# Spreading reciprocal roots over the partitions by transposition, and half 1's column sums by transposition and VectorE, in an encoder layer

## The chip, the cores and the metric

The kernel runs on one core of one Trainium2 chip. The metric is device time in microseconds (us). Lower is better. One profiled execution of the kernel before is at hand as well; all times below are microseconds from the start of its span unless they are marked ns.

## The reference

One layer of a bidirectional encoder over 1024 tokens of width 1024, in float32. What matters here are its two norms:

```
def rmsnorm(x, gain):
    xf = x.astype(jnp.float32)
    y = xf * lax.rsqrt(jnp.mean(xf * xf, axis=-1, keepdims=True) + EPS)
    return (y * gain.astype(jnp.float32)).astype(x.dtype)

h = rmsnorm(x, norm1_g) * (1.0 + sc1) + sh1
z = h @ w_in              # two branches (a gated MLP, a windowed attention) and two gates follow
...
x = x + gt1 * (merged @ w_o)
h2 = rmsnorm(x, norm2_g) * (1.0 + sc2) + sh2
f_gate, f_up = jnp.split(h2 @ w_ffn_in, 2, axis=-1)
x = x + gt2 * ((jax.nn.silu(f_gate) * f_up) @ w_ffn_out)
```

Each norm needs, for every token, the sum of the squares of its 1024 channels, the reciprocal root of their mean, and that root multiplied onto all 1024 channels of the token.

## The kernel before

The activations lie transposed: channels on the 128 partitions (eight tiles of 128 channels), tokens on the free axis. The 1024 tokens are worked in two halves of 512, by `half(0)` and `half(1)`; after them come the gates, the output projection, the second norm and the feed-forward part for both halves together. Nearly all products are "float32 as two parts": a high and a low part of each operand, three products (`mm3`: high by high, high by low, low by high).

Because channels lie on the partitions, the sum of squares of a token is a sum across partitions, and the root of a token must come back to all partitions. The steps of one norm for 512 tokens:

1. The squares of the eight channel tiles are added on ScalarE and VectorE into one 128 x 512 tile (`ss`).
2. `col_rstd` (line 381) takes the column sums on TensorE: for each of the four blocks of 128 tokens a float32 product with the block of `ss` as stationary operand and one column of ones as moving operand. A 128 x 4 tile comes out: token on the partition, block on the free axis.
3. `rstd` (line 375) turns it into the mean plus epsilon on VectorE (tile `ms`), and raises it to the power of minus one half on GpSimd (tile `rcol`).
4. `spread` (line 388) brings the root back to all partitions: for each block a float32 product whose stationary operand is the root's column repeated 128 times and whose moving operand is the identity. A 128 x 512 tile in PSUM comes out in which every partition holds all 512 roots.
5. VectorE multiplies the channel tiles with it (in `modulate`, line 409, and its like), ScalarE adds the shift and makes the high part, VectorE the low part.

The norms run at four places:

- **Norm 1 of half 0**, at the very start (lines 690 to 745). The column sums come there from products with a full tile of ones; the spread is written out, four float32 products into `rp`. Behind it in TensorE's program stand eight products for the condition's first column (`dot1`, into the bank `tot4`), then the projections' products. Half 0's attention window also reaches 128 tokens of the other half (the halo), which have a root of their own: `tot4[:, P : 2 * P]` at line 894 is its single product, issued ahead of the last pass of step k = 3; VectorE multiplies the halo's channels with it at k = 4 (`halo_four`).
- **Norm 1 of half 1**, inside half 0's last stage: the loop over d (eight tiles of output channels) with two groups of products j = 0, 1 per d, twelve matmuls each (lines 1169 to 1245). Behind group (4, 1) stands `col_rstd(ssn, NT, rcol[1])`, behind group (5, 0) `rb = spread(rcol[1], NT)`; in d = 5, 6, 7 `modulate` makes half 1's input from it.
- **Norm 2 of half 0** and **norm 2 of half 1**: column sums and `spread(rcol[2], NT)` out of a planner's list (lines 1780 to 1830; the planner, class `Plan`, orders operations by fixed costs, 0.45 for "few", the cost of a spread), and `col_rstd(sums[1], NT, rcol[3])` with `spread(rcol[3], NT)` among the first feed-forward products (lines 2153 to 2159).

Order: where `in_order[0]` is true, instructions keep their program order on each engine; elsewhere the framework's scheduler orders them (in half 0's last loop from d = 2 on, among other places). The last part runs under a manual schedule. TensorE, VectorE, ScalarE and GpSimd each work their queue in order.

The names in the profile: `at` and `mm` are the two sets of four PSUM banks, `mid`, `h`, `wh`, `wl`, `raw`, `t`, `ss`, `ms` SBUF tiles; all compute instructions carry line 144, a helper's line, and are told apart by tile names. `at<-ident,rcol` are the products of the spreads, `at<-ones,ss` the column sums, `at<-ident,lb`, `at<-ident,kd` and `at<-ident,mid` float32 transpositions that the kernel has elsewhere. A group's name gives the moving operand first, then the stationary one.

Of the kernel before, what the change touches and what calls it, by code (L numbers as in the profile page):

```python
# [16 lines left out]
P = 128  # L17
# [89 lines left out]
def kernel(  # L107
# [65 lines left out]
    def at_bank():  # L173
        return psum.tile([P, 512], F32, tag="at", name=nm("at"))
# [17 lines left out]
    def sm(n, name):  # L192
        return small.tile([P, n], F32, tag=name, name=nm(name))
# [184 lines left out]
        V.tensor_scalar(ms[:, :n], sums, 1.0 / D, EPS, op0=ALU.mult, op1=ALU.add)  # L378
        G.tensor_tensor(r[:, :n], ms[:, :n], nhalf[:, :n], op=ALU.pow)

    def col_rstd(ss, n, r):

        pt = at_bank()
        for i in range(n):
            T.matmul(pt[:, i : i + 1], ss[:, i * P : (i + 1) * P], ones[:, 0:1], start=True, stop=True)
        rstd(pt[:, :n], n, r)

    def spread(r, n):

        bc = at_bank()  # L390
        for i in range(n):
            T.matmul(bc[:, i * P : (i + 1) * P], r[:, i : i + 1].to_broadcast([P, P]), ident,
                     start=True, stop=True)
        return bc[:, : n * P]

    def ss_tile():
# [253 lines left out]
    def half(hf):  # L650
# [4 lines left out]
        if hf == 0:  # L655
            in_order[0] = True
            xt2 = [midt(F32, 4) for _ in range(2)]
            xt = [xt2[k // 4][:, k % 4, :] for k in range(KT)]
            halo = midt(F32, 16)
            xh, qh = halo[:, :KT, :], halo[:, KT:, :]  # L660
            hl4 = midt(F32R, 16)

            for k, n in ((0, 2), (2, 2), (4, 2), (6, 1), (7, 1)):
                load(xt2[k // 4][:, k % 4 : k % 4 + n, :].rearrange("p a b -> p (a b)"),
                     xA[:, k * HALF : (k + n) * HALF])
                if k == 2:
                    load_cond()
            hd_store = lambda q, f: f(
                hd[0, q * HALF : (q + 1) * HALF, :].rearrange("(a p) t -> p a t", p=P), xt2[q])
            load(cc[:, :80], cols)  # L670
            r = ada_pair(0)
            wq0, wk0 = (wpool.tile([P, UNIT], F32, tag="raw", name=nm("raw")) for _ in range(2))
            r1 = midt(F32, 2)
            load(r1[:, 0, :], blocks(w_ada1[1])[0])
            wq_half, wk_half = (blocks(w[0]) for w in (w_q, w_kv))
            load(wq0[:, :512], wq_half[0])
            load(wk0[:, :512], wk_half[0])
            load(r1[:, 1, :], blocks(w_ada1[1])[1])
            load(wq0[:, 512:], wq_half[1])
            base_bias = bias_base()  # L680
            A.activation(sm(QPK, "es"), ones[:, :QPK], AF.Silu)
            build_bias(*base_bias, range(BIAS))

            total = at_bank()
            open_bank(total, zeros, zeros)
            keep_going(total, zeros, zeros, ZEROS[0])
            cond = silu_rows()
            sqs = [midt(F32, 4) for _ in range(2)]
            sq = [sqs[k // 4][:, k % 4, :] for k in range(KT)]
            add = lambda i, j: V.tensor_tensor(sq[i], sq[i], sq[j], op=ALU.add)  # L690
            square = lambda k: A.activation(sq[k], xt[k], AF.Square)

            def square_dve(k):
                V.tensor_tensor(sq[k], xt[k], xt[k], op=ALU.mult)

            def column_sums(q, last=False):

                for i in range(NT):
                    T.matmul(total[:, i * P : (i + 1) * P], q[:, i * P : (i + 1) * P], ones,
                             start=False, stop=last and i == NT - 1)  # L700

            square(0)
            square(1)
            add(0, 1)
            column_sums(sq[0])
            square(2)
            square_dve(3)
            add(2, 3)
            column_sums(sq[2])
            square_dve(5)  # L710
            square(4)
            silu_cond(cond[:1])
            add(4, 5)
            column_sums(sq[4])
            square(6)
            square_dve(7)
            silu_cond(cond[1:], 1)
            A.activation(silu_col, ccol, AF.Silu)
            add(6, 7)
            column_sums(sq[6], True)  # L720
            root = sm(5, "ms")
            A.activation(root[:, :NT], total.rearrange("p (a b) -> p a b", b=P)[:, :, 0], AF.Sqrt, scale=1.0 / D, bias=epsc)
            wq, wk = ([wpool.tile([P, UNIT], F32R, tag=x, name=nm(x)) for x in ("wh", "wl")]
                      for _ in range(2))
            ada_dot(r[:, 0, :], SC1, then=ada_base)
            V.reciprocal(rcol[0][:, :NT], root[:, :NT])
            ada_dot(r[:, 1, :], SH1)
            rp = at_bank()
            kbk = [at_bank() for _ in range(2)]
            for bank in kbk:  # L730
                open_bank(bank, identr, zeros)
            keep_going(kbk[0], identr, zeros, ZEROS[1])
            for i in range(NT):
                T.matmul(rp[:, i * P : (i + 1) * P], rcol[0][:, i : i + 1].to_broadcast([P, P]), ident,
                         start=True, stop=True)
            tot4 = at_bank()

            dot1 = tot4[:, 2 * P : 3 * P]
            for i in range(KT):
                T.matmul(dot1, r1[:, 0, i * P : (i + 1) * P], silu_col[:, i : i + 1].to_broadcast([P, P]),  # L740
                         start=i == 0, stop=i == KT - 1)
            hH = [hid(), hid()]
            hL = [hid(), hid()]
        else:
            hH, hL = h_next
            in_order[0] = True
# [7 lines left out]
        for k in range(KT):  # L754
# [119 lines left out]
            for group in ((q_parts, k_parts) if hf == 1 and k == 4 else (q_parts + k_parts,)):  # L874


                if hf == 0:
                    if k == 4:
                        passes, late = [(e, q_parts) for e in range(3)], [(e, k_parts) for e in range(3)]
                    elif k == 0:  # L880
                        passes, late = [(0, group), (2, group), (1, q_parts)], [(1, k_parts)]
                    else:
                        passes, late = [(0, q_parts)] + late + [(0, k_parts), (1, group), (2, group)], []
                elif k == 0:

                    passes = [(e, part) for part in (q_parts[:3], q_parts[3:], k_parts) for e in (None, 2)]
                else:
                    passes = ((None, group), (2, group))
                for p, (e, part) in enumerate(passes):
                    if (hf, k, p) == (0, 2, 1):  # L890
                        for a in range(KT):
                            T.matmul(tot4[:, 0:1], qh[:, a, :], ones[:, 0:1], start=a == 0, stop=a == KT - 1)
                    elif (hf, k, p) == (0, 3, len(passes) - 1):
                        T.matmul(tot4[:, P : 2 * P], rcol[0][:, NT:].to_broadcast([P, P]), ident,
                                 start=True, stop=True)
                    for ps, st, w, o, n, first, last in part:
                        for e1 in ((0, 1) if e is None else (e,)):
                            T.matmul(ps, st[e1 // 2], w[e1 % 2][:, o : o + n],
                                     start=k + e1 == 0 and first,
                                     stop=bool(k == KT - 1 and e1 == 2 and last))  # L900
# [269 lines left out]
        for d in range(KT):  # L1170
# [24 lines left out]
            for j, (o, br) in enumerate(((512, (oH, oL)), (0, (gH, gL)))):  # L1195
                pb = mm_bank()
                for k in range(4):
                    kc = slice(o + k * P, o + (k + 1) * P)
                    mm3(pb, (wab[0][:, kc], wab[1][:, kc]),
                        (br[0][:, k, :], br[1][:, k, :]), k == 0, k == 3)  # L1200
                if hf == 0 and (d, j) == (4, 1):
                    col_rstd(ssn, NT, rcol[1])
                if hf == 0 and (d, j) == (5, 0):
                    rb = spread(rcol[1], NT)
                if d < PLAIN_GATES:
                    sg = sgs.pop(0)
                    V.scalar_tensor_tensor(out=sg, in0=sg, scalar=1.0, in1=pb, op0=ALU.add, op1=ALU.mult)
                    if (d, j) == (0, 0):
                        sums_of_w_o(3)
                    ms.append(sg)  # L1210
                else:
                    p = tmp()
                    A.copy(p, pb)
                    store(pd[hf, d, 1 - j], p)
# [1204 lines left out]
```

## Time and profile before

| | |
|---|---|
| median of 3 runs | 1214.48 us (1214.31 to 1214.61) |
| span of the profiled execution | 1212.9 us |
| median less span | 1.6 us |
| TensorE (PE) busy | 1206.9 us, 100% of the span, 5653 matmuls |
| TensorE weight loads (PEld) busy | 1007.5 us, 83% |
| VectorE (DVE) busy | 928.7 us, 77% |
| ScalarE (ACT) busy | 584.2 us, 48% |
| GpSimd (POOL) busy | 156.3 us, 13% |
| share of the 16 DMA engines | q1 39.5%, q0 16.2% |

The profile gives no time of its own for the profiled execution beside its span; the median of the runs lies 1.6 us above it. How to read it: a timeline's row gives start, duration, engine, line, operation, output tile and input tiles, shapes, the number of merged instructions and, in brackets, how long the engine had been idle before and what ended that. Matmuls overlap, so what a batch costs is the distance from its first start to the next group's start, not its duration. The chain of waits follows the end of the program back to its start, at each step to what released it.

### The profile page before, as it was taken

Reading aid. Unit: us, or ns where it says so; the run is one execution under the profiler, and the core shown is the slowest. Engines: PE = TensorE matmul, PEld = TensorE weight load, DVE = VectorE, ACT = ScalarE, POOL = GpSimd, SP = SyncE. Lnnn points to the kernel's source line nnn. Section 1 sums busy time; section 2 is a strip of 40 time slices with the busy share of each in tenths; the row PEclk is TensorE's granted clock in tenths of the full one; section 3 lists DMA queues with packets and bytes.
Section 4 is the critical chain, followed back from the end, with each engine's and each line's share of the span. In section 5 each row is a group of like instructions: output and inputs, shape, how many; then the busy total and the mean of one; then the engine's idle time right before and its main releaser. Section 6 shows DMA issues by size and latency. Waiting matters only on the chain.

```text
span 1212.9 us, 15658 instructions
## 1 busy us (share of the span) xinstructions
PE 1206.9 (100%) x5653; PEld 1007.5 (83%) x5653; DVE 928.7 (77%) x1505; ACT 584.2 (48%) x957; POOL 156.3 (13%) x190
## 2 busy tenths in 40 slices
PE   9999999999999999999999999999999999999998
PEld 7888888888888888888888888888888888888887
DVE  9999977889978886898987757676676765765646
ACT  5667865367855433745553333333333334433341
POOL 0024323024322000001000000010000000000001
PEclk9999999999999999999999999999999999999999
DMA  9743168753278543577213545554555449995552
GB/s 372 280 181 101 36 222 311 296 211 136 74 259 278 209 141 104 171 227 270 99 59 113 180 177 208 189 195 161 197 192 201 156 163 372 394 354 191 192 172 105
DMA packets 79713, 241.00 MB, mean 199 GB/s; under 512 B 9106, under 2 KB 9362, under 8 KB 74388
## 3 DMA queue, kind: packets, MB, share of 16 engines
q1 hardware_dynamic: 64004, 165.55, 39.5%
q0 software_dynamic: 15632, 74.46, 16.2%
q8 instruction: 44, 0.72, 0.2%
q14 instruction: 33, 0.27, 0.1%
HBM read 178.63 MB, written 61.34 MB: 198 GB/s over the span
## 4 chain that ended last, share of the span: by engine, by line
PE 99%; ACT 0%; DVE 0%; issue 0%; ACTq 0%
PE mm L144 50%; PE at L144 49%; DVE mid L144 0%; ACT mid L144 0%; ACT wh L144 0%; ACT h L144 0%; DVE crow L144 0%; ACT mod L144 0%; DVE zeros L144 0%; DVE ones L144 0%; DVE identr L144 0%; ACTq L144 0%
## 5 line engine op out<-in xcount | busy, mean ns | idle before, releaser
L144 ACT CAST wh<-raw 128x1024 fp32r<-128x1024 f32 (+1 forms) x154 | 157.1, 1021 | 110.7 <-PE mm L144 43.8
L144 DVE TENSOR_TENSOR wl<-raw,wh 128x1024 fp32r<-128x1024 f32 (+1 forms) x141 | 165.1, 1174 | 51.6 <-ACT wh L144 51.1
L144 PE MATMUL mm<-mid,wh 128*128 128x512 f32 x640 | 197.5, 390 | 0.0
L144 PEld LDWEIGHTS mm<-mid,wh 128*128 128x128 f32 x640 | 119.8, 188 | 24.7
L144 PE MATMUL mm<-wh,h 128*128 128x512 f32 x384 | 124.7, 396 | 0.2 <-ACT h L144 0.2
L144 PE MATMUL mm<-mid,wl 128*128 128x512 f32 x320 | 124.5, 389 | 0.0
L144 PE MATMUL mm<-h,wh 128*128 128x512 f32 x304 | 94.4, 391 | 0.0
L144 PE MATMUL at<-h,wh 128*128 128x512 f32 x304 | 93.8, 390 | 0.0
L144 PEld LDWEIGHTS mm<-wh,h 128*128 128x128 f32 x384 | 70.8, 188 | 13.9 <-ACT h L144 0.4
L144 DVE TENSOR_TENSOR wl<-ws,wh 128x1024 fp32r<-128x1024 f32 (+1 forms) x50 | 55.8, 1117 | 24.1 <-ACT wh L144 24.1
L144 PE MATMUL mm<-wl,h 128*128 128x512 f32 x192 | 71.2, 391 | 0.0
L144 PEld LDWEIGHTS mm<-mid,wl 128*128 128x128 f32 x320 | 60.1, 188 | 12.5
L144 PEld LDWEIGHTS at<-h,wh 128*128 128x128 f32 x304 | 56.9, 188 | 11.7
L144 ACT CAST wh<-ws 128x1024 fp32r<-128x1024 f32 (+1 forms) x50 | 48.3, 967 | 37.3 <-DVE ws L144 24.9
L144 PEld LDWEIGHTS mm<-h,wh 128*128 128x128 f32 x304 | 56.6, 188 | 11.6
L144 ACT ACTIVATE t<-t 128x512 f32<-128x512 f32 x46 | 28.4, 630 | 70.8 <-DVE t L144 70.8
L144 DVE TENSOR_TENSOR ol<-raw,oh 128x1024 fp32r<-128x1024 f32 x30 | 36.6, 1223 | 31.1 <-ACT oh L144 31.1
L144 PE MATMUL mm<-h,wl 128*128 128x512 f32 x152 | 59.2, 390 | 0.0
L144 PE MATMUL at<-h,wl 128*128 128x512 f32 x152 | 59.1, 389 | 0.0
L144 ACT ACTIVATE xs<-xs 128x512 f32<-128x512 f32 x21 | 13.3, 633 | 93.6 <-DVE xs L144 93.6
L144 ACT CAST oh<-raw 128x1024 fp32r<-128x1024 f32 x30 | 31.6, 1055 | 44.3 <-PE at L144 23.0
L144 PE MATMUL at<-wl,wh 128*128 128x512 f32 (+1 forms) x136 | 52.7, 388 | 0.0
(300 smaller groups left out, 2883.9 us busy)
## 6 DMA issues: line engine op xcount, KB each, us to landing
mid<-in_w_ada_dram SPq DMA_DIRECT2D x30, 512.0 KB, 7.4
raw<-in_w_gate_dram SPq DMA_DIRECT2D x26, 512.0 KB, 3.6
tA<-hid POOLq DMA_DIRECT2D x11, 1024.0 KB, 5.1
tB<-hid POOLq DMA_DIRECT2D x11, 1024.0 KB, 5.2
wo<-in_w_out_dram POOLq DMA_DIRECT2D x22, 512.0 KB, 6.1
wS<-wo POOLq DMA_DIRECT2D x11, 1024.0 KB, 5.2
raw<-wS SPq DMA_DIRECT2D x44, 256.0 KB, 3.5
raw<-tB SPq DMA_DIRECT2D x44, 256.0 KB, 5.0
```

Source lines behind the costliest of these rows:

```text
L144: ins = f(*args, **kw)
```

## The change

`T.transpose` takes the place of the float32 product in all spreads: in `spread`, in the one written out for `rp`, and in the halo's single one. It has the same operands: the root's repeated column, and the identity. That is 17 products of 128 x 128 in all (four in `rp`, one in `tot4`, four in each of three spreads).

Half 1's column sums are no longer products with ones. `turned` transposes the four 128 x 128 blocks of `ssn` into a PSUM bank, `summed` adds each block's 128 elements per partition by a `tensor_reduce` on VectorE (tile `cs`), and `rstd` reads that. The other column sums stay products. The spread of half 1's root is moved: from behind group (5, 0) to behind the first three matmuls of group (5, 1).

```diff
+    def turned(ss, n):
+
+        pt = at_bank()
+        for i in range(n):
+            T.transpose(pt[:, i * P : (i + 1) * P], ss[:, i * P : (i + 1) * P], ident)
+        return pt
+
+    def summed(pt, n):
+
+        s = sm(5, "cs")
+        V.tensor_reduce(out=s[:, :n], in_=pt[:, : n * P].rearrange("p (a b) -> p a b", b=P), axis=AX.X,
+                        op=ALU.add)
+        return s[:, :n]
+
-    def col_rstd(ss, n, r):
+    def col_rstd(ss, n, r, by_turning=False):

+        if by_turning:
+            rstd(summed(turned(ss, n), n), n, r)
+            return
         pt = at_bank()
         for i in range(n):
             T.matmul(pt[:, i : i + 1], ss[:, i * P : (i + 1) * P], ones[:, 0:1], start=True, stop=True)
...
         bc = at_bank()
         for i in range(n):
-            T.matmul(bc[:, i * P : (i + 1) * P], r[:, i : i + 1].to_broadcast([P, P]), ident,
-                     start=True, stop=True)
+            T.transpose(bc[:, i * P : (i + 1) * P], r[:, i : i + 1].to_broadcast([P, P]), ident)
         return bc[:, : n * P]
...
             for i in range(NT):
-                T.matmul(rp[:, i * P : (i + 1) * P], rcol[0][:, i : i + 1].to_broadcast([P, P]), ident,
-                         start=True, stop=True)
+                T.transpose(rp[:, i * P : (i + 1) * P], rcol[0][:, i : i + 1].to_broadcast([P, P]), ident)
...
-                        T.matmul(tot4[:, P : 2 * P], rcol[0][:, NT:].to_broadcast([P, P]), ident,
-                                 start=True, stop=True)
+                        T.transpose(tot4[:, P : 2 * P], rcol[0][:, NT:].to_broadcast([P, P]), ident)
...
+                    if hf == 0 and (d, j, k) == (5, 1, 0):
+                        rb = spread(rcol[1], NT)
                 if hf == 0 and (d, j) == (4, 1):
-                    col_rstd(ssn, NT, rcol[1])
-                if hf == 0 and (d, j) == (5, 0):
-                    rb = spread(rcol[1], NT)
+                    col_rstd(ssn, NT, rcol[1], True)
```

## The prediction

> **What bounds the kernel now.** I read the page first, for the bound of the whole, and then the waits of TensorE's two queues.
>
> ```profile
> span 1212.9 us, 15658 instructions
> ...
> PE 99%; ACT 0%; DVE 0%; issue 0%; ACTq 0%
> ...
> PE at L144 <- DVE identr L144: 1.9, 1, 1.9
> PE mm L144 <- ACT h L144: 0.2, 1, 0.2
> ```
>
> The chain that ended last is TensorE for 99% of the span, and TensorE waits twice: 1.9 us before its first matmul, and 0.2 us for ScalarE's `h`. So each matmul that goes away is worth its place in TensorE's stream, unless another engine is just as late at that point. The change removes only matmuls from the stream. Two questions remain: what is a transposition worth against a product, and where does TensorE, come earlier, meet something that doesn't come earlier with it?
>
> The price is read from timelines, as the distance from one group's first start to the next group's. Half 1's column sums and its spread:
>
> ```profile
> 188.51 0.94 PE L144 MATMUL at<-ones,ss 128*128 128x1 f32 x8
> 189.31 0.72 PE L144 MATMUL mm<-mid,wh 128*128 128x512 f32 x2
> ...
> 189.49 0.16 DVE L144 TENSOR_SCALAR ms<-at 128x4 f32<-128x4 f32 x1 [2.74 <-PE at L144]
> 189.57 1.23 DVE L144 TENSOR_TENSOR wl<-raw,wh 128x1024 fp32r<-128x1024 f32 x1
> ...
> 189.74 1.96 POOL L144 TENSOR_TENSOR rcol<-ms,nhalf 128x4 f32<-128x4 f32 x1 [2.17 <-DVE ms L144]
> ...
> 192.18 1.05 PE L144 MATMUL at<-ident,rcol 128*128 128x128 f32 x8
> 192.99 0.71 PE L144 MATMUL mm<-mid,wh 128*128 128x512 f32 x2
> ```
>
> Four float32 products are eight instructions, two passes each. The column sums hold the stream from 188.51 to 189.31, 0.80 us, and the spread from 192.18 to 192.99, 0.81 us: 0.10 us a pass, with one column as with 128. The kernel's own transpositions of float32 blocks, four of `kd` and sixteen of `mid`, with the group behind each:
>
> ```profile
> 66.03 0.60 PE L144 MATMUL at<-ident,kd 128*128 128x128 f32 x4
> 66.39 0.47 PE L144 MATMUL mm<-wh,h 128*128 128x512 f32 x1
> ```
>
> ```profile
> 159.40 2.04 PE L144 MATMUL at<-ident,mid 128*128 128x128 f32 x16
> 161.19 0.71 PE L144 MATMUL mm<-mid,wh 128*128 128x512 f32 x2
> ```
>
> ```profile
> L144 PE MATMUL at<-ident,lb x176: 270/273/332, 87.6 to 325.8; 128*128 128x128 f32 x176
> ```
>
> Four take 0.36 us, and sixteen 1.79, 0.11 each. They are one instruction each, with the same shapes and the same moving operand as the spread. So a batch of four gives back 0.81 - 0.36 = 0.45 us, and a single one one pass, 0.11. The longer duration, 0.27, matters only for who reads the result.
>
> The Trainium skill ("FP8 and Floating Point Precision", TensorE Precision Notes) counts four passes through the array for true float32. By it a transposition would be worth a quarter of a product, four would take 0.81 / 4 = 0.20 us, and each batch would give back 0.61. The rows of `kd` say 0.36; the measurement decides.
>
> **The change, part by part.** At the start, four products become transpositions (`rp`):
>
> ```profile
> 12.95 1.16 PE L144 MATMUL at<-ident,rcol 128*128 128x128 f32 x8
> ...
> 13.93 0.08 DVE L144 DVE_READ_ACCUMULATOR mid<-mid,silu_c 128x1 f32 x1
> 13.95 1.95 PE L144 MATMUL at<-cc,mid 128*128 128x128 f32 x16
> ...
> 14.24 0.75 DVE L144 SCALAR_TENSOR_TENSOR mid<-mid,mod,at 128x512 f32<-128x512 f32 x1 [0.22 <-PE at L144]
> ...
> 15.08 0.72 ACT L144 ACTIVATE h<-mid,mod 128x512 fp32r<-128x512 f32 x1 [0.73 <-DVE mid L144]
> ...
> 15.85 1.19 PE L144 MATMUL mm<-wh,h 128*128 128x512 f32 x4
> ```
>
> TensorE is through 0.45 earlier, but the first projection product at 15.85 needs `h`, which comes by VectorE (14.24) and ScalarE (15.08). VectorE finishes its last instruction at 14.01 and starts at 13.94 at the earliest, as its instructions overlap by 0.07. So this place passes on 14.24 - 13.94 = 0.30 at most. The `dot1` products end by 15.40 and cover the rest.
>
> The halo's root is next:
>
> ```profile
> 32.29 1.21 DVE L144 TENSOR_TENSOR wl<-raw,wh 128x1024 fp32r<-128x1024 f32 x1
> ...
> 33.17 0.38 PE L144 MATMUL at<-ident,rcol 128*128 128x128 f32 x2
> ```
>
> ```profile
> 33.59 0.70 DVE mid L144
> ...
> 34.31 1.66 ACT mid L144 x4
> ...
> 38.74 0.73 ACT h L144
> ...
> 39.52 1.20 PE mm L144 x4
> ```
>
> The second fence is the chain of waits between 33 and 40 us. TensorE's one wait on the page, for `h` at 39.52, goes back through ScalarE and VectorE to this product: it ends at 33.55, VectorE starts at 33.59. As a transposition, 0.30 earlier, it ends at 32.87 + 0.27 = 33.14, and VectorE can start at 33.18. VectorE itself is free at 33.43 - 0.30 = 33.13. So the chain gains 0.40, and so does TensorE at 39.52. Of the 0.56 us removed until then (0.45 + 0.11) 0.40 arrive; the other 0.16 lengthen the wait for `h`.
>
> Half 1's column sums give back 0.80 - 0.36 = 0.44. A wait is added in front of the root: VectorE's sum over 512 elements. The trace has a sum of 512 elements per partition from SBUF, none from PSUM:
>
> ```profile
> L144 DVE TENSOR_REDUCE qms<-t x8: 672/678/681, 58.9 to 245.3; 128x8 f32<-128x512 f32 x8
> ```
>
> I take 0.68 us; below nothing is excluded, since it is a new instruction, and the upper bound is an instruction of 1024 elements, the 1.23 us of `wl`, with which the root would come 0.55 later than reckoned here and TensorE would wait 0.18. VectorE had been idle for 2.74 us before `ms`, so nothing hinders the start. Queued behind it stands the `wl` of 189.57, which serves products of the loop's end, more than 10 us later. The times, on the old clock from 188.51: the last transposition starts at 188.84 and ends at 189.12; the sum runs from 189.16 to 189.84, `ms` to 190.00, GpSimd's power, at its longest of 1.96, from 190.09 to 192.05. Column sums shortened by 0.44, twelve matmuls (192.18 - 189.31 = 2.87) and the three of the move (0.68, three times 0.227) bring TensorE to the spread at 188.87 + 2.87 + 0.68 = 192.42. The root is 0.37 early; it was 0.48 early (191.70 against 192.18). Nobody waits. The spread ends 0.45 shorter, so VectorE's `modulate` has its roots at about 193.0, where it had them at 193.23. On GpSimd's queue one store of `pd` stands behind the power and moves by 0.35; its buffer is one of four. If the root came late all the same, TensorE would wait with the rest of (5, 1) behind it.
>
> Half 1's spread gives back 0.45. The two later ones keep their column sums and order:
>
> ```profile
> 561.19 1.05 PE L144 MATMUL at<-ident,rcol 128*128 128x128 f32 x8
> ...
> 561.39 0.75 DVE L144 SCALAR_TENSOR_TENSOR mid<-mm,ngt,mid 128x512 f32<-128x512 f32 x1 [1.56 <-PE mm L144]
> 562.28 2.72 DVE L144 SCALAR_TENSOR_TENSOR mid<-mid,mod,at 128x512 f32<-128x512 f32 x4
> ...
> 583.18 0.69 DVE L144 TENSOR_TENSOR ss<-ss,t 128x512 f32<-128x512 f32 x1 [0.16 <-ACT t L144]
> ...
> 583.65 0.39 PE L144 MATMUL at<-h,wl 128*128 128x512 f32 x1
> 584.02 1.02 PE L144 MATMUL at<-ones,ss 128*128 128x1 f32 x8
> ...
> 587.73 1.05 PE L144 MATMUL at<-ident,rcol 128*128 128x128 f32 x8
> ```
>
> From 562.28 on VectorE runs without a pause until `ss` is done at 583.87, and the next column sums wait for that: 584.02, where 0.23 behind 583.65 would be 583.88. VectorE starts this stretch when the spread is done; free at 562.07, it can gain 0.21 of the 0.45. So TensorE gets 0.21 here, and the wait at 584 grows by 0.24; if the stretch has slack that I don't see, it gets all 0.45. The last spread (587.73) gives 0.45 with nothing late behind it.
>
> The sum: 0.40 + 0.44 + 0.45 + 0.21 + 0.45 = 1.95 us. The span goes from 1212.9 to about 1210.9, the median, 1.58 above the span, from 1214.48 to 1212.5. The bounds: all 21 passes (17 and 4) at 0.11 would be 2.3, and 1212.2; losing also the start's 0.40 gives 1.55, and 1212.9.
>
> **The rivals.**
>
> - *The root comes late.* If the scheduler, which orders VectorE in this loop, puts `wl` between the sum and `ms`, or in front of both, the root comes 1.14 later (1.23 less the overlap of about 0.09) and TensorE stands still for 1.14 - 0.37 = 0.77 at the longest power. In the old order `ms` went first although `wl` was ready 0.08 later; that speaks against. Time 1213.3.
> - *The gain is spent in half 1.* VectorE is busy 77% of the span, TensorE runs 1.3 earlier from 200 us on, and a stretch paced by VectorE or a load would take part of it back. Against it: the waits name no such stretch on TensorE. Half of 1.95 lost: 1213.5.
> - *Nothing changes:* a transposition of a repeated column still issues two passes. The rows of `kd` speak against; the time would be 1214.5.
> - *A transposition costs less than `kd`'s.* Its stationary operand is one column read over and over; at half of `kd`'s 0.11 a batch of four would hold the stream 0.2 less, on the three batches that nothing absorbs 0.6 in all: 1211.9. No row shows less than 0.11. The Trainium skill's count of passes, above, would make it so.
> - *Slower: transpositions don't keep the array's clock up.* At the start of the program TensorE was slow:
>
> ```profile
> 1.86 4.63 PE L144 MATMUL at<-zeros 128*128 128x512 f32 x10 [1.86 <-DVE identr L144]
> ...
> 8.65 1.61 PE L144 MATMUL at<-ones,mid 128*128 128x128 f32 x13
> ```
>
> Ten matmuls took 4.63, about 0.46 each, against 0.227 later, and full pace is reached at 8.65, after 6.8 us. If a batch of transpositions sent the array back into such a stretch, half of 6.8, 3.4 us, would be lost, more than the whole gain from the first batch on: 1215.9 for one, near 1229.5 for all five. Against it: sixteen transpositions in a row at 159.40 are followed at once by matmuls at full pace. The Trainium skill ("TensorE: Matmul & The Clock Gate", Part 4: PE-mode transpose) says that the full clock doesn't engage for transpose mode, at about 275 ns a transposition. The trace agrees with the duration (273 ns), and not with its use as a cost: 0.11 apart.
>
> **How the numbers follow.** The forecast, 1212.5 within 0.4, has 0.66; a late root 0.11; a gain spent in half 1 0.09; a cheaper transposition 0.06; no change 0.03; the clock, slower, 0.05. What a measurement of this kernel can tell from no change is about 0.2%, 2.4 us, so the border of faster is at 1212.05. The cheaper transposition and the forecast's lower edge (0.06 + 0.07) make faster 0.13; slower is the clock and a little for a worse order of the loop, 0.06; the same gets 0.81. The range reaches from the cheaper transposition to a gain half spent with some margin, 1211.8 to 1213.9.
>
> **What would show it.** In the changed profile: four `at<-ident,rcol` instructions in each spread, the next group 0.36 behind; `at<-ident,ss` four times near 188; a VectorE sum of 0.68 us, `ms` right behind it, and `rcol` done about 0.4 ahead of the spread; a longer wait for `h` near 39, and one of about 0.4 before the column sums near 582. It is wrong if TensorE waits before the moved spread, if the batches stay at 0.8, or if matmuls behind a batch last longer than 0.39.

## The result and the profile after

| | before | after |
|---|---|---|
| median, same chip, 5 runs each | 1214.61 us (1214.31 to 1216.2) | 1220.83 us (1220.73 to 1221.37) |
| span of the profiled execution | 1212.9 us | 1218.8 us |
| ratio after to before | | 1.0051 (95%: 1.004 to 1.0061) |

The change makes the kernel slower by about 6.2 us; 2 us less were forecast. I read the same views as before the change: the page's first line and its chain (the chain of work that ended last), then the waits of TensorE's queue, both of the kernel after.

```profile
span 1218.8 us, 15616 instructions
...
PE 97%; DVE 2%; ACT 0%; DMA 0%; issue 0%; DVEq 0%; ACTq 0%
```

```profile
PE at L144 <- DVE identr L144: 1.9, 1, 1.9
PE mm L144 <- ACT h L144: 0.2, 1, 0.2
```

TensorE is still the bound, and its two waits are the two of before with the same sizes. So the 6 us are no wait; they must lie inside TensorE's own stream. The first spread and then half 1's norm, in the timeline of the kernel after (start, duration, engine, operation, tiles, in brackets the idle time before):

```profile
12.43 0.65 PE L144 MATMUL at<-ident,rcol 128*128 128x128 f32 x4
...
187.60 0.60 PE L144 MATMUL at<-ident,ss 128*128 128x128 f32 x4
187.96 0.71 PE L144 MATMUL mm<-mid,wh 128*128 128x512 f32 x2
188.24 0.69 DVE L144 TENSOR_REDUCE cs<-at 128x4 f32<-128x512 f32 x1 [2.16 <-PE at L144]
...
188.85 1.22 DVE L144 TENSOR_TENSOR wl<-raw,wh 128x1024 fp32r<-128x1024 f32 x1
...
189.98 0.16 DVE L144 TENSOR_SCALAR ms<-cs 128x4 f32<-128x4 f32 x1
...
190.23 1.04 POOL L144 TENSOR_TENSOR rcol<-ms,nhalf 128x4 f32<-128x4 f32 x1 [0.30 <-DVE ms L144]
...
191.48 0.60 PE L144 MATMUL at<-ident,rcol 128*128 128x128 f32 x4
191.83 0.71 PE L144 MATMUL mm<-mid,wh 128*128 128x512 f32 x2
```

Both batches of half 1 hold the stream 0.36 and 0.35 us, where they held it 0.80 and 0.81. Here everything still goes by the forecast: before's group behind the spread started at 192.99, three products earlier in the loop (0.68 us), so TensorE is 192.99 + 0.68 - 191.83 = 1.84 us ahead, 0.5 of it because this execution was that much earlier already at the change's first instruction (12.43 against 12.95). At the next spread the lead is gone:

```profile
561.48 0.60 PE L144 MATMUL at<-ident,rcol 128*128 128x128 f32 x4
561.84 0.48 PE L144 MATMUL mm<-b22h,wh 128*128 128x512 f32 x1
```

Before, this spread started at 561.19. Without a single wait TensorE has lost 1.84 + 0.29 = 2.1 us between 192 and 561 us, in a stretch in which the change edits nothing. How many products start in equal stretches shows the same for the rest of the program. The columns are the window, busy time, TensorE's busy time with the count, the granted clock, the DMA share and GB/s; before, then after:

```profile
600.00:800.00 200.00, 200.00 (x884) 1.00 0.42 150
800.00:1000.00 200.00, 200.00 (x884) 1.00 0.51 182
1000.00:1200.00 200.00, 200.00 (x884) 1.00 0.73 261
```

```profile
600.00:800.00 200.00, 200.00 (x871) 1.00 0.42 150
800.00:1000.00 200.00, 200.00 (x872) 1.00 0.49 176
1000.00:1200.00 200.00, 200.00 (x882) 1.00 0.73 260
```

TensorE is 100% busy in both, at a granted clock of 1.00 in both, and in 200 us it starts 13 and 12 products fewer: by 0.227 these are 2.9 and 2.7 us, until about 1000 us; after that it is 2 products. "Busy 100%" hides it, since overlapping products count as busy however far apart they start. The single starts show which products it is. TensorE's timeline in the feed-forward block, before and then after:

```profile
649.18 0.39 PE L144 MATMUL at<-tt2h,wh 128*128 128x512 f32 x1
649.40 0.39 PE L144 MATMUL at<-tt2l,wh 128*128 128x512 f32 x1
649.63 0.39 PE L144 MATMUL at<-tt2h,wl 128*128 128x512 f32 x1
...
651.22 0.62 PE L144 MATMUL mm<-mid,wh 128*128 128x512 f32 x2
651.67 0.39 PE L144 MATMUL mm<-mid,wl 128*128 128x512 f32 x1
```

```profile
649.77 0.39 PE L144 MATMUL at<-tt2h,wh 128*128 128x512 f32 x1
650.00 0.40 PE L144 MATMUL at<-tt2l,wh 128*128 128x512 f32 x1
650.24 0.39 PE L144 MATMUL at<-tt2h,wl 128*128 128x512 f32 x1
...
651.87 0.63 PE L144 MATMUL mm<-mid,wh 128*128 128x512 f32 x2
652.33 0.39 PE L144 MATMUL mm<-mid,wl 128*128 128x512 f32 x1
...
652.56 0.62 PE L144 MATMUL mm<-mid,wh 128*128 128x512 f32 x2
...
653.92 0.62 PE L144 MATMUL mm<-mid,wh 128*128 128x512 f32 x2
```

From 649.18 to 651.22 nine products take 2.04 us, 0.227 each. From 649.77 to 651.87 the same nine take 2.10, 0.233 each. Behind them, with `mid` as the moving operand, three products still take 0.69 (651.87 to 652.56), 0.23 each, and then the distance comes back: the six from 652.56 to 653.92 take 1.36, 0.227 each. Taken over all pairs of starts, the products that move `tt1h`, `tt1l`, `tt2h`, `tt2l`, `b22h` or `b22l` lie 232.1 to 233.3 ns apart after, and 226.5 to 227.0 before. There are 1152 of them; by 6.1 ns that is 7.0 us. Some 790 products that move `mid` behind 380 us lie 227.7 ns apart instead of 226.6, and 48 that move `h` against a stationary tile of the feed-forward block 232.4 instead of 226.7; they add 1.1 us.

All the slow tiles come from one pool, that of the feed-forward block. What the change did to that pool stands in no timeline, but in the memory map of the two compiled programs. `cs` is a new tag in the pool of small tiles: four slots of 20 bytes, each rounded up to 32, so 128 bytes in each partition. Each pool that is allocated behind it moves up by 128. `tt1h` starts at byte 175,424 of the partition before and at 175,552 after; `wh` (32,064), `wl` (44,352), `h` (56,640) and `mid` (89,408) stay. Before, all of these starts leave 64 when divided by 256; after, the feed-forward tiles leave 192.

### The profile page after: what moved, and what is told of

Its sections match the earlier page's. It is cut to its first block, busy times and chain, and to the rows that moved or that the text cites. A ratio compares the mean times of both kernels' runs of the same rounds, so it can differ in the third digit from the quotient of the medians.

```text
span 1218.8 us, 15616 instructions
## 1 busy us (share of the span) xinstructions
PE 1212.7 (99%) x5632; PEld 1004.6 (82%) x5632; DVE 929.7 (76%) x1506; ACT 583.7 (48%) x957; POOL 155.3 (13%) x190
## 4 chain that ended last, share of the span: by engine, by line
PE 97%; DVE 2%; ACT 0%; DMA 0%; issue 0%; DVEq 0%; ACTq 0%
PE mm L144 49%; PE at L144 48%; DVE mid L144 1%; DVE wl L144 0%; DMA mid<-in_xA_dram 0%; ACT mid L144 0%; DVE h L144 0%; ACT wh L144 0%; ACT h L144 0%; DVE wh L144 0%; ACT mod L144 0%; ACT ms L144 0%; DVE rcol L144 0%; DVEq L144 0%; ACTq L144 0%
## 5 line engine op out<-in xcount | busy, mean ns | idle before, releaser
L144 PE MATMUL at<-wh,wl 128*128 128x512 f32 (+1 forms) x136 | 52.8, 388 | 0.0
```

What stands on the lines that cost most here:

```text
L144: ins = f(*args, **kw)
```

## The experiments

**The theory** (A, where an expectation has letters): the change's own steps give what was forecast, and the loss is the place of the feed-forward tiles, moved by the new tile: a product is slower when its moving operand lies otherwise, modulo 256 bytes (in the rest that its start leaves when divided by 256), than its stationary one. **The rivals:** the change's instructions (transpositions, VectorE's sum, the order that the scheduler gives them) slow the stream behind them; or places matter, but the moving operand's own place does, or that of the one pool, whatever the weights' is.

**The change on the old places.** The sum is written into the old tag `ms` instead of a new one, and nothing else is different.

```diff
-        s = sm(5, "cs")
+        s = sm(5, "ms")
```

> The change as it is, but the VectorE sum's result tile takes a slot of the ms tiles instead of a tag of its own, so that no SBUF tile lies elsewhere than before the change. Theory A (the new 128 bytes moved the later pools, and the products whose moving operand lies there go 6 ns apart more): the slowdown is gone and the local gains remain, 1214.6 - 2.0 = 1212.6, within 0.5; matmuls 0.227 apart from 350 us on. Theory B (the scheduler's new order, or TensorE's shorter program, makes the slowdown): about 1220.8, as after the change.

1212.6 us, against 1214.57 for the kernel before on the same chip: 0.9985 (0.9976 to 0.9994). All instructions of the change are there, and the loss is gone.

**The kernel before on the new places.** An unused tile in the pool of small tiles, 128 bytes, and the same with 256 and 64. None holds an instruction of the change.

```diff
+            G.memset(small.tile([P, 32], F32, tag="pad", name="pad", bufs=1), 0.0)
             attention_constants()
```

> The kernel before, with one unused tile of 128 bytes a partition in the pool of small tiles, written once by GpSimd at about 50 us; TensorE's program is that of before. Theory A: the whole slowdown without the change, 1214.6 + 7.7 = 1222.3, within 1.0; matmuls with a moving operand of the tt1, tt2, b22 and first tiles 0.233 apart. Theory B: 1214.6.

> The kernel before, with an unused tile of 256 bytes. Under theory A it tells the step: if places repeat every 256 bytes 1214.6, if any distance from the old place counts or places repeat every 512 or more, between 1218 and 1225. Theory B: 1214.6.

> The kernel before, with an unused tile of 64 bytes. Under theory A: if only multiples of 64 bytes matter to the port that reads, 1214.6; if the moving operand's place against the stationary operand's counts in any step, 1218 to 1225. Theory B: 1214.6.

With 128 bytes: 1222.71 us, 1.0067 (1.0053 to 1.0081). With 256: 1214.44, 0.9999 (0.999 to 1.0008). With 64: 1221.68, 1.0057 (1.0044 to 1.0071). An unused tile of 128 bytes costs 8.1 us, and one of 256 bytes nothing. With the first experiment this leaves the change's instructions no part of the loss. With 64 the theory fits less closely. The products of the feed-forward block then lie 229.8 ns apart on average, those that move `tt1l` only 226.5, as if nothing had moved; about half of the 7.1 us lies in them. Most of the rest is in products that move `mid` behind them (230.2 ns), whose own two places agree. The kernel before with 128 bytes shows the slower pace in its `tt1h` products (count, then shortest, median and longest duration in ns); the first fence is the kernel before itself:

```profile
L144 PE MATMUL at<-tt1h,wh x112: 389/389/389, 394.2 to 990.5; 128*128 128x512 f32 x112
```

```profile
L144 PE MATMUL at<-tt1h,wh x112: 391/394/404, 394.1 to 998.1; 128*128 128x512 f32 x112
```

**Which place counts.** All pools behind the constants move by 128 bytes together, the weights too (the unused tile stands in the pool of constants, which is allocated first):

```diff
+            G.memset(const.tile([P, 32], F32, tag="pad", name="pad", bufs=1), 0.0)
             attention_constants()
```

> The kernel before, with an unused tile of 128 bytes a partition in the pool of constants, which is allocated first: the weights, h, mid and the feed-forward tiles all move by 128 bytes, and their places against one another stay. If the slower products come from the place of the moving operand against the stationary one (modulo 256 bytes), nothing changes: 1214.6 us, 0.2267 us between products. If the place of the moving operand itself counts, modulo 256, then all products with mid, h or a feed-forward tile as the moving operand go to 0.233 us: 1152 with mid, 912 with h and 1152 of the feed-forward block by 6.5 ns make 21 us, 1235. If it is the feed-forward pool's own place alone: 1222.3.

1214.79 us, 1.0002 (0.9993 to 1.0011): nothing.

```profile
L144 PE MATMUL at<-tt1h,wh x112: 389/389/390, 393.8 to 990.3; 128*128 128x512 f32 x112
```

`tt1h` starts at the same byte as in the slow kernels, 175,552, and its products are at full pace, since the weights have moved as well. Both forms of the rival "its own place" fall. Then `mid` and all behind it move against the weights and `h` (the tile stands in the pool of `h`):

```diff
+            G.memset(hpool.tile([P, 32], F32, tag="pad", name="pad", bufs=1), 0.0)
             attention_constants()
```

> The kernel before, with the unused 128 bytes behind h, so that mid is moved as well as the feed-forward tiles, against the weights (and h) that stay. If any moving operand that lies off its stationary one by 128 bytes modulo 256 is slow, the 1152 products with mid as the moving operand lose 6.5 ns each beside the 1152 of the feed-forward block, 7.5 us each: 1229.5 us. If the loss belongs to the feed-forward pool alone, 1222.5.

1229.58 us, 1.0125 (1.011 to 1.0141). The products that move `mid`, between 600 and 1000 us, first in the kernel before and then here:

```profile
L144 PE MATMUL at<-mid,wh x128: 389/389/389, 624.0 to 960.8; 128*128 128x512 f32 x128
```

```profile
L144 PE MATMUL at<-mid,wh x128: 390/393/404, 630.2 to 974.6; 128*128 128x512 f32 x128
```

They have become slow in the same way (233 ns from start to start), and the cost is that of 1152 more products: 1229.58 - 1222.71 = 6.9 us beside the feed-forward block's 8.1. It is no property of one pool.

The Trainium skill ("SBUF — State Buffer", SBUF: two separate sides) says that on the engines' side only the port pair that VectorE and GpSimd share causes contention. The run in which all moved and the one in which `mid` moved agree as far as they reach: the work of the other engines is the same in both, and only the second is slow. That speaks against contention between engines, and for the places of TensorE's own two operands.

**A smaller offset.** 32 unused bytes in the pool of small tiles of the kernel before.

> The kernel before, with 32 unused bytes in the pool of small tiles: the feed-forward tiles begin 32 bytes off the weights, modulo 256. If every offset that is no multiple of 256 is slow, 1221.7 to 1222.7 us as with 64 and 128; if only multiples of 64 are, or the loss grows with the offset, 1214.6 or some 1218.

1225.7 us, 1.0092 (1.0078 to 1.0106), 3 us more than was expected of every offset.

```profile
L144 PE MATMUL at<-tt1h,wh x112: 393/396/400, 394.0 to 1000.0; 128*128 128x512 f32 x112
```

So an offset of 32 bytes is not harmless but the worst of those tried. The products of the feed-forward block lie 232.4 to 234.5 ns apart. The rest is elsewhere: those that move `mid` behind 380 us lie 229.3 apart (226.6 before), though `mid` and the weights had not moved.

**One part of the change alone.** The spreads by transposition, half 1's column sums by products as before, and so no `cs`.

```diff
-                    col_rstd(ssn, NT, rcol[1], True)
+                    col_rstd(ssn, NT, rcol[1])
```

> The change without its column sums by transposition (half 1's are formed by products against ones, as before), and so without the new tile, all else as in the change. If the steps of the sum are right and the loss comes from the new tile's place alone: the gain of the change on the old places less 0.44, so 1214.57 - 1.51 = 1213.1 us, all products 0.2267 apart. If the transposed spreads themselves slow what follows them, over 1219.

1213.2 us, 0.999 (0.9981 to 0.9998). As expected, within 0.1; the part that is left out is worth 0.6 by the medians, 0.44 by the step. The moved spread stands in its timeline as in the change's:

```profile
191.98 0.60 PE L144 MATMUL at<-ident,rcol 128*128 128x128 f32 x4
192.34 0.71 PE L144 MATMUL mm<-mid,wh 128*128 128x512 f32 x2
```

**The change with its tile, on places 256 bytes further.** The new tag gets eight slots in place of four.

```diff
-        s = sm(5, "cs")
+        s = small.tile([P, 5], F32, tag="cs", name=nm("cs"), bufs=8)
```

> The change as it is, its new tile with it, but with eight slots for that tile in place of four, so that the pools behind it move by 256 bytes and not by 128. If only the places behind the new tile cost the time, 1212.6 us as with the tile's sums put into an old tile, and the products of the feed-forward block are 0.2267 apart. If the new tile or the order that the scheduler gives with it costs something of its own, it shows here and not there: over 1213.5.

1212.74 us, 0.9987 (0.9978 to 0.9996). Its `tt1h` products are those of the kernel before:

```profile
L144 PE MATMUL at<-tt1h,wh x112: 389/389/389, 392.6 to 988.2; 128*128 128x512 f32 x112
```

The tile and the scheduler's order cost nothing; 1220.83 - 1212.74 = 8.1 us are the places. This kernel, the one with the sum in `ms` and the one with the spreads alone (1213.2) are the three that beat both the kernel before and the change.

## Why the prediction was wrong

The forecast's local steps can be read off the last experiment's trace, where the places don't disturb them. At 12 us this execution ran 0.27 ahead of the one of before, which is taken off. Its rows, in order of time (the first number in a fence is the start):

```profile
12.68 0.65 PE L144 MATMUL at<-ident,rcol 128*128 128x128 f32 x4
...
38.84 1.21 PE L144 MATMUL mm<-wh,h 128*128 128x512 f32 x4 [0.17 <-ACT h L144]
```

```profile
559.61 0.60 PE L144 MATMUL at<-ident,rcol 128*128 128x128 f32 x4
559.97 0.48 PE L144 MATMUL mm<-b22h,wh 128*128 128x512 f32 x1
```

```profile
581.61 0.39 PE L144 MATMUL at<-h,wl 128*128 128x512 f32 x1
582.09 1.02 PE L144 MATMUL at<-ones,ss 128*128 128x1 f32 x8
...
585.82 0.60 PE L144 MATMUL at<-ident,rcol 128*128 128x128 f32 x4
586.17 0.71 PE L144 MATMUL at<-h,wh 128*128 128x512 f32 x2
```

- **Start and halo**, forecast 0.40: the product behind the wait for `h` came at 39.52 and comes at 38.84, so 0.68 - 0.27 = 0.41. Right. The longer wait for `h` did not come (0.17, and it was 0.2): the prediction had let 0.45 of the start reach this point, though by its own step only 0.30 passes the first projection product.
- **Half 1's column sums**, forecast 0.44: 187.96 - 187.60 = 0.36 in the change, so 0.44. VectorE's sum took 0.69 (0.68 forecast). Right.
- **The root's lead**, forecast 0.37: 0.21 (190.23 + 1.04 = 191.27, spread at 191.48). The scheduler did put `wl` between the sum and `ms`, the order of the rival "the root comes late". It cost nothing, because GpSimd's power took 1.04 and not the 1.96 reckoned with; at 1.96 TensorE would have waited about 0.7. The shorter power comes with that order. In the kernel before `wl` ran on VectorE beside the power, which ended 0.90 behind it (190.80 to 191.70); where no `wl` ran beside it, here and at 586.30 in the kernel before, it took 1.04. So that rival was overpriced: it counted the later start and the long power together.
- **Half 1's spread** and **the last one**, forecast 0.45 each: they hold the stream 0.35, and held it 0.81. Right.
- **Norm 2 of half 0**, forecast 0.21: the spread gives 0.45 (0.36 held), and the distance in front of the next column sums is 0.48 where it was 0.37, so the wait grew by 0.11 and not by 0.24. 0.34 remain; VectorE's stretch had the slack that the prediction left open. In the change itself this wait is missing, as TensorE comes later there.

Together about 2.1 us by this trace. The medians of the two kernels that have the whole change and keep the places modulo 256 lie 1.7 and 2.0 under the kernel before, around the 1.95 of the sum.

**The step that failed** is the added tile. The sum rests on "The change removes only matmuls from the stream". The prediction priced `cs` by its VectorE instruction and by who waits for it, and let all other products keep their 0.227 us. It never asked what the tile does to the memory map. That term was set at 0 and measures 8.1 us, four times the whole gain. The prediction had a rival on the slower side, with a wrong mechanism: a clock lost behind transpositions. Two runs rule it out as the cause: all transpositions on the old places take 1212.6 us, and the kernel before, without any of the new ones, takes 1222.71 with 128 unused bytes. The granted clock is 1.00 in all windows of after shown above. The Trainium skill ("TensorE: Matmul & The Clock Gate", Part 4: PE-mode transpose) says that the full clock doesn't engage in transpose mode; no run here shows an effect of that. One of its marks did fire, products longer than 0.39 us, but not behind a batch: they are those of the feed-forward block from about 390 us on, 200 us after half 1's batch.

What is not settled: why the places of TensorE's two operands against each other matter. The runs show what it depends on, not how it works inside. They don't tell either whether a product's own stationary operand counts or the next one's, whose weight load starts with it (both at 649.18 in the kernel before): nearly everywhere here both lie at the same offset.

## What to carry to other kernels

A new small tile is not free even if nobody waits for it: it moves every pool allocated behind it, and with products back to back the place of the moving operand against the stationary one is part of the price. After such an edit compare the tiles' starts of the two memory maps, and put the tile into an existing slot or round the addition up to 256 bytes. When a change of a few instructions moves the time by microseconds and no wait has grown, count the starts in equal windows far from the edit before looking at the edit.

## What the runs showed of the hardware

- The moving operand's place against the stationary one's, modulo 256 bytes, changes the pace of back-to-back products of 128 x 512 elements. Equal, in the feed-forward block: 0.2267 us from start to start. Its tiles 128 bytes off: 0.233, for the most part in a pattern of 229 and 238 ns in turn; 64 off: 0.2298 on average, with some products at full pace. What such an offset cost the kernel before: 11.2 us with 32 bytes, 7.1 with 64, 8.1 with 128, nothing measurable with 256 (-0.1).
- The disturbance outlasts the operands that cause it: in the change three products that move `mid` behind a feed-forward group still lie 230 to 233 ns apart, though their own places agree. With an offset of 64 it is about ten products, at 224 to 236.
- All of it goes on at 100% busy and a granted clock of 1.00; only starts, counts and the longest durations (404 ns against 389) tell it. The granted clock doesn't tell the pace the other way round either: in the profiled execution of the kernel with the sum in `ms` it was 0.95 from start to end, and the products of the feed-forward block lay 0.2267 us apart.
- GpSimd's power of 128 x 4 elements took 1.04 us with no `wl` on VectorE beside it, and up to 1.96 beside one; then it ended 0.90 us behind that `wl`. Why was not tested.
